# A two-layer SSD and mLSTM trunk on one core: how rows reach all partitions, and how modulation sums are taken

## The chip, the core and the metric

One core of a Trainium2 chip runs the whole program. The metric is device microseconds of one execution. Three executions of the kernel before were timed, and one was profiled.

## What is computed

The input is a residual stream of 256 tokens by 2048 channels and one conditioning vector `c`. There are two layers. Each one computes a modulation from `c`, applies an RMS norm with it, projects in, mixes tokens, projects out, gates and adds.

```
cond = silu(c)
for i in range(2):
    mod = cond @ ada_w[i] + ada_b[i]            # 2048 x 6144, one row
    shift, scale, gate = split(mod, 3)
    h = rmsnorm(x, norm_w[i]) * (1 + scale) + shift
    out = ssd_mixer(h, ...) if i == 0 else mlstm_mixer(h, ...)
    x = x + gate * out
return rmsnorm(x, final_norm_w)
```

The SSD mixer needs, for each of 64 heads, `exp(acs[t] - acs[s])` for all pairs of tokens of a chunk, where `acs` is a running sum over tokens. The mLSTM mixer needs `exp` of a like difference for each of 8 heads, and then `num = (q k^T * decay) @ v` with 512 value columns per head. All values are fp32.

## The kernel before, in words

Channels lie on the partitions (128) and tokens along the free axis (256). A weight tile of 128 x 2048 comes by a DMA from SyncE in two halves (`raw`, 512 KB each, six buffers). ScalarE rounds a half to `hi` (helper `act`, L73), VectorE takes the rest as `lo` (helper `vtt`, L81), and TensorE multiplies hi by hi, hi by lo and lo by hi (L253 to L255, or L264 to L266 for the value projection). A half is 24 matmuls of 256 columns. The buffers `hi` and `lo` are four each.

A list `items` fixes the order: weight tiles (`w`), modulation tiles (`a`) and norm chunks (`h`). For each half, the loop at the end prepares the next three halves (`prep`: loads, splits, modulation work, norm chunks), steps background work (`run_bg`) and then issues the matmuls. Background work is a list of Python generators, `gens`. One call of `run_bg` advances each of them to its next `yield`, and stops early after five of them when a tally of VectorE or ScalarE work is too high. `finish` steps all of them, whatever the tally, until the ones that it names are over. The framework then places the instructions on each engine's queue by the order of the source and its own model of durations, so the order on an engine can differ from the source's. Each engine's queue is run in order.

Modulation (`ada_work`): each of 12 groups of 1024 columns is accumulated by VectorE in `aacc` (L77, 16 steps; one buffer). Then, in the source directly behind the last step, TensorE transposes each of 8 blocks of 128 columns (L202), and ScalarE copies the transposed block onto itself with a running sum, which gives 8 columns of `asum`; the transposes of four blocks share one PSUM bank. VectorE adds the bias.

SSD (`gen_ssd`, one generator for each of 8 groups): `rows(j)` brings four rows of `acs` (1 KB each) to partition 0 of a tile `acb` by four DMAs from GpSimd (L567), and a GpSimd `partition_broadcast` copies them to all partitions (L569). `decay(j)` makes `E` of it on ScalarE. VectorE multiplies by `cbm`, TensorE multiplies with `X` (L612, L613). Then the squares of the result are summed for each token, GpSimd raises the sum to the power -0.5 (`stat_to_bcast`, L280, tile `rs`), VectorE spreads it to a diagonal-ready tile `dg`, and TensorE transposes it (`bcast`, L289). An output projection over groups begins with `finish` of these groups.

mLSTM (`gen_ml`, one for each of 8 heads): one row `G` goes the same way (L814, L815) to `Gb`. The value product (L848, L850) runs in four steps of two matmuls into a bank each, each followed by one VectorE operation (L77) and a `yield`.

The final norm's weights come by one DMA of a row and one `partition_broadcast` for each half (L320, L321).

Of the kernel before, what the change touches and what calls it, by code (L numbers as in the profile page):

```python
# [8 lines left out]
F32 = mybir.dt.float32  # L9
# [37 lines left out]
def trunk_kernel(ctx, tc, xt, vecs, ada, wdt, wss, wso, wgt, wml, wmo, fnw, result):  # L47
# [5 lines left out]
    sp = ctx.enter_context(tc.tile_pool(name="sp", bufs=2))  # L53
    pj = ctx.enter_context(tc.tile_pool(name="pj", bufs=4, space=PS))
    pm = ctx.enter_context(tc.tile_pool(name="pm", bufs=4, space=PS))

    uid = [0]

    def nm(s):
        uid[0] += 1  # L60
        return f"{s}{uid[0]}"
# [9 lines left out]
    def act(out, in_, func, **kw):  # L71
        charge("a", out, 0.833e-3, 0.1 + 0.09 * sum(isinstance(kw.get(k), bass.AP) for k in ("bias", "scale")))
        nc.scalar.activation(out, in_, func, **kw)  # L73

    def stt(out, a, s, b, op0, op1):
        charge("v", out, 1.04e-3, 0.07 + 0.06 * isinstance(s, bass.AP))
        nc.vector.scalar_tensor_tensor(out, a, s, b, op0, op1)  # L77

    def vtt(out, a, b, op):
        charge("v", out, 1.04e-3, 0.07)  # L80
        nc.vector.tensor_tensor(out, a, b, op)  # L81
# [16 lines left out]
    def vec(n, i=0, w=1):  # L98
        o, _ = VOFF[n]
        return V[:, o + i:o + i + w]  # L100
# [70 lines left out]
            run_bg()  # L171

    acc_tiles = {}
    known = set()

    def ada_work(it):
        layer, key, q, w = it["layer"], it["key"], it["q"], it["w"]
        per = 1024 // w
        if q == 0:
            acc_tiles[layer, key] = sp.tile([P, 1024], F32, tag="adaacc", name=nm("aacc"), bufs=1)  # L180
        acc = acc_tiles[layer, key][:, 0:w]
        for k in range(2 * per * q, 2 * per * (q + 1)):
            raw = it["raw"][(k // per) % 2][:, (k % per) * w:(k % per + 1) * w]
            if k == 0:
                vts(acc, raw, cond[:, 0:1], None, ALU.mult)
            else:
                stt(acc, raw, cond[:, k:k + 1], acc, ALU.mult, ALU.add)
        if q != it["nq"] - 1:
            return
        if isinstance(key, tuple):  # L190
            spans = [(4 * key[0] + 2 * key[1] + 16 * j, 2) for j in range(2)]
        elif key < 4:
            spans = [(4 * key, 4), (16 + 4 * key, 4)]
        else:
            spans = [(32 + 8 * (key - 4), 4), (36 + 8 * (key - 4), 4)]
        sm = sp.tile([P, 8], F32, tag="asum", name=nm("asum"))
        c = 0
        for o, n in spans:
            ps = misc()
            for b in range(n):  # L200
                sl = slice(b * P, (b + 1) * P)
                nc.tensor.transpose(ps[:, sl], acc[:, c * P:(c + 1) * P], ident)  # L202
                act(ps[:, sl], ps[:, sl], AF.Copy, accum_out=sm[:, c:c + 1])
                c += 1
            m = mod[layer][:, o:o + n]
            vtt(m, sm[:, c - n:c], vec(f"ab{layer}", o, n), ALU.add)
            known.update((layer, o + b) for b in range(n))
            if 16 <= o < 32:
                stt(amul[layer][:, o - 16:o - 16 + n], m, 1.0, vec(f"nw{layer}", o - 16, n), ALU.add, ALU.mult)

    def load(it):
        it["raw"] = {}
# [65 lines left out]
    def stat_to_bcast(v):  # L278
        r = sp.tile([P, 2], F32, tag="rs", name=nm("rs"))
        nc.gpsimd.tensor_tensor(r, v, nhalf, ALU.pow)  # L280
        return r
# [33 lines left out]
    class OutStat(RowStat):  # L315
        def prepare(self):
            self.w = []
            for i in range(2):
                w = sp.tile([P, 4, T], F32, tag="a4", name=nm("fnw")).rearrange("p b t -> p (b t)")
                nc.gpsimd.dma_start(w[0:1, :], fnw[:, 1024 * i:1024 * (i + 1)])  # L320
                nc.gpsimd.partition_broadcast(w, w[0:1, :])  # L321
                self.w.append(w)
            self.o = [wp.tile([P, D], F32, tag="y", name=nm("o"), bufs=4) for _ in range(2)]

# [146 lines left out]

    passes = set()

    # ------------------------------------------------------------ layer 0
    st0 = RowStat()
    for u in range(4):
        st0.add(u)
# [2 lines left out]
    dtT = cp.tile([P, 2, 64], F32, tag="dtT", name="dtT")  # L480
    acT = cp.tile([P, 3, 64], F32, tag="acT", name="acT")
    acs = cp.tile([P, T], F32, tag="rowA", name="acs")
    dsk = cp.tile([P, 32], F32, tag="dskh", name="dskh")
    vts(dsk, vec("dsk", 0, 32), 0.5, None, ALU.mult)
    cbm = {}
# [2 lines left out]
    def dt_done(banks):  # L488
        def g():
            bk = banks[0][:, 0:T]  # L490
            rw = sp.tile([P, 4, T], F32, tag="a4", name="dtrow")
            dt, tmp = rw[:, 0, :], rw[:, 1, :]
            vts(tmp, bk, vec("dtb"), None, ALU.add)
            softplus(tmp, dt)
            yield
            na = sp.tile([P, 1], F32, tag="na", name="na", bufs=1)
            act(na, vec("alog"), AF.Exp)
            vts(na, na, -1.0, None, ALU.mult)
            vts(tmp, dt, na, None, ALU.mult)
            for c in range(2):  # L500
                s = slice(c * P, (c + 1) * P)
                nc.vector.tensor_tensor_scan(acs[:, s], ones, tmp[:, s], 0.0, ALU.mult, ALU.add)
            cr = tmp[:, 0:P]
            vts(cr, acs[:, 0:P], -1.0, acs[:, P - 1:P], ALU.mult, ALU.add)
            yield
            p1, p2 = misc(), misc()
            for c in range(2):
                nc.tensor.transpose(p1[:, c * P:(c + 1) * P], dt[:, c * P:(c + 1) * P], ident)
                nc.tensor.transpose(p2[:, c * P:(c + 1) * P], acs[:, c * P:(c + 1) * P], ident)
            nc.tensor.transpose(p2[:, 2 * P:3 * P], cr, ident)  # L510
            vts(dtT, p1[:, 0:T].rearrange("p (c h) -> p c h", c=2)[:, :, 0:64],
                                    0.5, None, ALU.mult)
            nc.vector.tensor_copy(acT, p2[:, 0:384].rearrange("p (c h) -> p c h", c=3)[:, :, 0:64])
            yield
        held["dt"] = spawn(g())
# [44 lines left out]
    def gen_ssd(g):  # L560
        acb, E = [None, None], [None, None]

        def rows(j):
            acb[j] = sp.tile([P, 4, T], F32, tag="a4", name=nm("acb"))
            h0 = 8 * g + 4 * j
            for h in range(4):
                nc.gpsimd.dma_start(acb[j][0:1, h, :], acs[h0 + h:h0 + h + 1, :])  # L567
            fl = acb[j].rearrange("p h t -> p (h t)")
            nc.gpsimd.partition_broadcast(fl, fl[0:1, :])  # L569

        def decay(j):
            e = E[j] = sp.tile([P, 4, 384], F32, tag="e6", name=nm("E"))
# [60 lines left out]
        token_sq(xs, [v[:, tb:tb + 1] for tb in range(2)])  # L633
        vts(v, v, 1.0 / 512, 4 * EPS, ALU.mult, ALU.add)
        r = stat_to_bcast(v)
        yield
        rb = bcast(r)
        yield
# [100 lines left out]
        out.extend(extra[e:])  # L739
        items[start:] = out  # L740

    # ------------------------------------------------------------ layer 1
    m1 = len(items)
    eT = cp.tile([P, 2, 8], F32, tag="eT", name="eT")
    ncT = cp.tile([P, 2, 8], F32, tag="ncT", name="ncT")
    G = cp.tile([P, T], F32, tag="rowA", name="G")
    mnw = cp.tile([P, 32], F32, tag="mnwh", name="mnwh")
    vts(mnw, vec("mnw", 0, 32), 0.5, None, ALU.mult)

    def gates_done(banks):  # L750
        def g():
# [15 lines left out]
            nc.vector.tensor_tensor_scan(bc, for_scan, lf, 0.0, ALU.mult, ALU.add)  # L767
            vtt(ip, ip, bc, ALU.subtract)
            nc.vector.tensor_tensor_scan(G, ip, ip, 0.0, ALU.max, ALU.max)
            vtt(lf, bc, G, ALU.add)  # L770
            yield
            p1, p2 = misc(), misc()
# [38 lines left out]
    def gen_ml(h):  # L811
        yield from gate_ok(lambda: "gates" in held and held["gates"].over)
        Gb = sp.tile([P, T], F32, tag="gb", name=nm("Gb"))
        nc.gpsimd.dma_start(Gb[0:1, :], G[h:h + 1, :])  # L814
        nc.gpsimd.partition_broadcast(Gb, Gb[0:1, :])  # L815
        yield
        EP = sp.tile([P, 2, 384], F32, tag="e6", name=nm("EP"))
        e, pp = EP[:, 0, :], EP[:, 1, :]
# [24 lines left out]
        yield  # L843
        yield from gate_ok(lambda: h in v_t and h in to_t)
        v, to = v_t[h], to_t[h]
        for b in range(4):
            ps = misc()
            nc.tensor.matmul(ps[:, 0:T], v[:, 0, b * P:(b + 1) * P], pp[:, 0:T], start=True, stop=False,  # L848
                             skip_group_check=True)
            nc.tensor.matmul(ps[:, P:T], v[:, 1, b * P:(b + 1) * P], pp[:, T:384], start=False, stop=True,  # L850
                             skip_group_check=True)
            stt(to[:, b, :], to[:, b, :], 1.0, ps[:, 0:T], ALU.add, ALU.mult)
            yield
        ss = sp.tile([P, 2], F32, tag="ss2", name=nm("ss2"))
        sq = sp.tile([P, 4, T], F32, tag="e6", name=nm("sq"))
# [57 lines left out]
    add_out_pass(1, (6, 7), st2, True, st2.prepare, wmo, after=st2.write)  # L913
    interleave(m1, [a for cc in (4, 5) for a in ada_items(1, cc)], upto=40)

    # ------------------------------------------------------------ run
    halves = []
    for n, it in enumerate(items):
        if it["kind"] == "w":
# [8 lines left out]
    def prep(j):  # L928
        n, half = halves[j]
        it = items[n]  # L930
        if it["kind"] == "h":
            for k in it["ks"]:
                h_chunk(it["layer"], k)
            return
        while nload[0] < min(len(loads), it["ln"] + LOOK_LOAD):
            load(loads[nload[0]])
            nload[0] += 1
        if it["kind"] == "a":
            ada_work(it)
        else:  # L940
            with prio(*HP_SPLIT):
                split(it, half)
# [108 lines left out]
```

## Time and profile before

| | |
|---|---|
| median of three executions | 1790.29 us |
| the three | 1785.38, 1790.29, 1799.31 us |
| span of the profiled execution, first to last instruction | 1784.4 us |
| median less span | 5.9 us |
| TensorE busy | 1696.1 us |
| VectorE busy | 1295.9 us |
| ScalarE busy | 923.6 us |
| GpSimd busy | 97.4 us |
| mean granted TensorE clock | 0.979 of full |

The profiled execution's own time is its span and what lies around it; the table puts the latter at the difference to the median. A matmul's end is modelled and overlaps the next one's start, so busy shares are upper bounds of useful work, and the pace is read from starts.

### The profile page before, as it was taken

The numbers are of one execution on the slowest core, as the hardware profiler recorded it, in microseconds if no ns is written. First come the engines' busy times: TensorE is split into PE (matmuls) and PEld (weight loads), VectorE is DVE, ScalarE is ACT, GpSimd is POOL, SyncE is SP. The second block draws the span as 40 slices with busy tenths as digits, with TensorE's granted clock in tenths as the row PEclk, the third lists the DMA queues.
The fourth block names the chain that finished last, engine by engine and source line by source line (L and its number), as shares of the span: only waits on it lengthen the run. The fifth ranks groups of instructions, "written<-read, shape, count | busy, mean of one in ns | idle before, by whom it ended". The sixth has DMA issues, their size and how long they took to land.

```text
span 1784.4 us, 32951 instructions
## 1 busy us (share of the span) xinstructions
PE 1696.1 (95%) x13285; PEld 1633.0 (92%) x13285; DVE 1295.9 (73%) x1615; ACT 923.6 (52%) x1571; POOL 97.4 (5%) x127
## 2 busy tenths in 40 slices
PE   2999999999899899899999999999999999999997
PEld 2998999999899889899898989899989898989996
DVE  6789899999886789886777776646455555564554
ACT  3443557998553487445455445544345454454442
POOL 0000003222200020000000000000000000000000
PEclk6999999999999999999999999999999999999998
DMA  9988856566776885894666676545555555554551
GB/s 359 327 305 300 291 183 209 184 201 219 264 247 219 276 298 193 295 339 167 230 227 235 235 259 209 188 169 186 184 183 173 181 171 184 175 180 170 185 178 71
DMA packets 110377, 394.74 MB, mean 221 GB/s; under 512 B 14352, under 2 KB 14352, under 8 KB 110224
## 3 DMA queue, kind: packets, MB, share of 16 engines
q1 hardware_dynamic: 107856, 392.54, 64.5%
q8 instruction: 104, 1.70, 0.4%
q0 software_dynamic: 2368, 0.09, 0.1%
q14 instruction: 49, 0.40, 0.1%
HBM read 390.41 MB, written 2.10 MB: 220 GB/s over the span
## 4 chain that ended last, share of the span: by engine, by line
PE 68%; DVE 11%; issue 11%; DMA 5%; ACT 3%; POOL 1%; SPq 0%; ACTq 0%; POOLq 0%; DVEq 0%
PE pj L253 16%; PE pj L254 16%; PE pj L255 16%; DVE aacc L77 4%; DVE lo L81 4%; PE pj L264 3%; PE pj L265 3%; PE pj L266 3%; DMA raw<-in_ada 3%; PE ms L253 2%; PE ms L254 2%; PE ms L255 2%; ACT hi L73 1%; DMA raw<-in_wss 1%; PE ms L202 1%
## 5 line engine op out<-in xcount | busy, mean ns | idle before, releaser
L73 ACT ACTIVATE hi<-raw 128x1024 fp32r<-128x1024 f32 x548 | 580.9, 1062 | 719.9 <-PE pj L254 496.8
L81 DVE TENSOR_TENSOR lo<-raw,hi 128x1024 fp32r<-128x1024 f32 x548 | 670.0, 1225 | 321.9 <-ACT hi L73 318.9
L253 PE MATMUL pj<-hT,hi 128*128 128x256 f32 x2400 | 683.8, 285 | 4.3 <-ACT hT L73 4.3
L254 PE MATMUL pj<-hT,hi 128*128 128x256 f32 x2400 | 676.4, 282 | 0.5 <-DVE hT L77 0.5
L255 PE MATMUL pj<-hT,lo 128*128 128x256 f32 x2400 | 674.6, 281 | 1.3 <-DVE lo L81 1.3
L253 PEld LDWEIGHTS pj<-hT,hi 128*128 128x128 f32 x2400 | 456.7, 191 | 5.7 <-ACT hT L73 4.9
L254 PEld LDWEIGHTS pj<-hT,hi 128*128 128x128 f32 x2400 | 456.7, 190 | 1.7 <-issue 0.8
L255 PEld LDWEIGHTS pj<-hT,lo 128*128 128x128 f32 x2400 | 455.8, 190 | 2.1 <-DVE lo L81 1.7
L253 PE MATMUL pj<-y,hi 128*128 128x256 f32 x1024 | 292.2, 285 | 0.0
L254 PE MATMUL pj<-y,hi 128*128 128x256 f32 x1024 | 291.8, 285 | 0.0
L255 PE MATMUL pj<-y,lo 128*128 128x256 f32 x1024 | 291.4, 285 | 0.0
L77 DVE SCALAR_TENSOR_TENSOR aacc<-raw,cond,aacc 128x1024 f32<-128x1024 f32 x180 | 236.0, 1311 | 40.4 <-DMA raw<-in_ada 38.8
L253 PEld LDWEIGHTS pj<-y,hi 128*128 128x128 f32 x1024 | 197.2, 193 | 0.6 <-issue 0.3
L254 PEld LDWEIGHTS pj<-y,hi 128*128 128x128 f32 x1024 | 197.4, 193 | 0.0
L255 PEld LDWEIGHTS pj<-y,lo 128*128 128x128 f32 x1024 | 197.2, 193 | 0.0
L253 PE MATMUL ms<-hT,hi 128*128 128x256 f32 x448 | 127.2, 284 | 2.3 <-DVE park L81 2.0
L255 PE MATMUL ms<-hT,lo 128*128 128x256 f32 x448 | 126.2, 282 | 0.8 <-DVE lo L81 0.8
L254 PE MATMUL ms<-hT,hi 128*128 128x256 f32 x448 | 126.2, 282 | 0.0
L264 PE MATMUL pj<-hi,hT 128*128 128x512 f32 x256 | 101.8, 398 | 0.0
L265 PE MATMUL pj<-hi,hT 128*128 128x512 f32 x256 | 101.4, 396 | 0.0
L266 PE MATMUL pj<-lo,hT 128*128 128x512 f32 x256 | 101.2, 395 | 0.0
L253 PEld LDWEIGHTS ms<-hT,hi 128*128 128x128 f32 x448 | 85.2, 190 | 3.5 <-DVE park L81 2.6
(175 smaller groups left out, 1557.9 us busy)
## 6 DMA issues: line engine op xcount, KB each, us to landing
raw<-in_wml SPq DMA_DIRECT2D x256, 512.0 KB, 4.0
raw<-in_ada SPq DMA_DIRECT2D x192, 512.0 KB, 5.2
raw<-in_wss SPq DMA_DIRECT2D x160, 512.0 KB, 4.9
raw<-in_wso SPq DMA_DIRECT2D x64, 512.0 KB, 5.1
raw<-in_wmo SPq DMA_DIRECT2D x64, 512.0 KB, 3.6
xT<-in_xt SPq DMA_DIRECT2D x4, 512.0 KB, 6.2
out<-o SPq DMA_DIRECT2D x4, 512.0 KB, 4.0
raw<-in_wdt SPq DMA_DIRECT2D x2, 512.0 KB, 3.1
```

What stands on the lines that cost most here:

```text
L73: nc.scalar.activation(out, in_, func, **kw)
L77: nc.vector.scalar_tensor_tensor(out, a, s, b, op0, op1)
L81: nc.vector.tensor_tensor(out, a, b, op)
L202: nc.tensor.transpose(ps[:, sl], acc[:, c * P:(c + 1) * P], ident)
L253: nc.tensor.matmul(o, hi[:, w0:w0 + P], ah, start=first, stop=False, skip_group_check=True)
L254: nc.tensor.matmul(o, hi[:, w0:w0 + P], al, start=False, stop=False, skip_group_check=True)
L255: nc.tensor.matmul(o, lo[:, w0:w0 + P], ah, start=False, stop=last, skip_group_check=True)
L264: nc.tensor.matmul(o, ah[:, s], wh, start=(k == 0), stop=False)
L265: nc.tensor.matmul(o, al[:, s], wh, start=False, stop=False)
L266: nc.tensor.matmul(o, ah[:, s], wl, start=False, stop=(k == u.ktot - 1))
```

## The change

- `rows(j)`: the scan's result is written once to a DRAM scratch `acd`. One DMA from GpSimd per `j` then reads four rows of it and writes them to all 128 partitions (512 KB). The same for `G` with a scratch `Gd` (128 KB per head), and for the final norm's weights from the input itself. All uses of `partition_broadcast` on GpSimd are gone.
- Modulation sums: a background generator, spawned when a group of columns is accumulated. Its first step does nothing; its second step issues 8 matmuls with a block of `aacc` as weights and one column of ones as the moving side, and VectorE adds the bias from PSUM. `finish(sums)` stands ahead of the next group's first accumulation and ahead of each norm chunk.
- SSD: one more `yield` between `stat_to_bcast` and `bcast`.
- mLSTM value products: all eight matmuls of a head are issued in one step into two banks; after a `yield`, VectorE takes two operations of 512 columns with a `yield` behind each, in place of four of 256.

```diff
+    dr = ctx.enter_context(tc.tile_pool(name="dr", bufs=1, space=bass.MemoryType.DRAM))
...
         if q == 0:
+            finish(sums)
             acc_tiles[layer, key] = sp.tile([P, 1024], F32, tag="adaacc", name=nm("aacc"), bufs=1)
...
-        sm = sp.tile([P, 8], F32, tag="asum", name=nm("asum"))
-        c = 0
-        for o, n in spans:
+        def total():
+            yield
             ps = misc()
-            for b in range(n):
-                sl = slice(b * P, (b + 1) * P)
-                nc.tensor.transpose(ps[:, sl], acc[:, c * P:(c + 1) * P], ident)
-                act(ps[:, sl], ps[:, sl], AF.Copy, accum_out=sm[:, c:c + 1])
-                c += 1
-            m = mod[layer][:, o:o + n]
-            vtt(m, sm[:, c - n:c], vec(f"ab{layer}", o, n), ALU.add)
...
+            c = sum(n for _, n in spans)
+            for b in range(c):
+                nc.tensor.matmul(ps[:, b:b + 1], acc[:, b * P:(b + 1) * P], ones[:, 0:1], start=True, stop=True)
+            c = 0
+            for o, n in spans:
+                m = mod[layer][:, o:o + n]
+                vtt(m, ps[:, c:c + n], vec(f"ab{layer}", o, n), ALU.add)
...
+        sums.append(spawn(total()))
...
-                nc.gpsimd.dma_start(w[0:1, :], fnw[:, 1024 * i:1024 * (i + 1)])
-                nc.gpsimd.partition_broadcast(w, w[0:1, :])
+                nc.gpsimd.dma_start(w, fnw[:, 1024 * i:1024 * (i + 1)].partition_broadcast(P))
...
+            nc.gpsimd.dma_start(acd, acs[0:64, :])
...
-            for h in range(4):
-                nc.gpsimd.dma_start(acb[j][0:1, h, :], acs[h0 + h:h0 + h + 1, :])
-            fl = acb[j].rearrange("p h t -> p (h t)")
-            nc.gpsimd.partition_broadcast(fl, fl[0:1, :])
+            nc.gpsimd.dma_start(acb[j].rearrange("p h t -> p (h t)"),
+                                acd[h0:h0 + 4, :].rearrange("(o h) t -> o (h t)", o=1).partition_broadcast(P))
...
         r = stat_to_bcast(v)
+        yield
         yield
         rb = bcast(r)
...
+            nc.gpsimd.dma_start(Gd, G[0:8, :])
...
-        nc.gpsimd.dma_start(Gb[0:1, :], G[h:h + 1, :])
-        nc.gpsimd.partition_broadcast(Gb, Gb[0:1, :])
+        nc.gpsimd.dma_start(Gb, Gd[h:h + 1, :].partition_broadcast(P))
...
+        pv = [misc(), misc()]
         for b in range(4):
-            ps = misc()
-            nc.tensor.matmul(ps[:, 0:T], v[:, 0, b * P:(b + 1) * P], pp[:, 0:T], start=True, stop=False,
+            o = pv[b // 2][:, T * (b % 2):T * (b % 2) + T]
+            nc.tensor.matmul(o, v[:, 0, b * P:(b + 1) * P], pp[:, 0:T], start=(b % 2 == 0), stop=False,
...
-            stt(to[:, b, :], to[:, b, :], 1.0, ps[:, 0:T], ALU.add, ALU.mult)
+        yield
+        for i in range(2):
+            stt(to[:, 2 * i:2 * i + 2, :], to[:, 2 * i:2 * i + 2, :], 1.0, pair(pv[i]), ALU.add, ALU.mult)
             yield
...
         if it["kind"] == "h":
+            finish(sums)
```

## Rows read from the trace of the kernel before

**Rows 1.** Busy time by stretch: length, engines, granted clock, DMA share, GB/s.
```profile
400.00:450.00 50.00, 48.92 (x415) 47.41 (x415) 49.31 (x67) 43.69 (x109) 10.75 (x12) 1.00 0.66 224
...
900.00:1750.00 850.00, 849.84 (x6423) 812.25 (x6422) 517.40 (x642) 396.59 (x514) 16.92 (x24) 1.00 0.57 192
```

**Rows 2.** Waits of TensorE's matmuls, 45 to 1700 us: total us, times, longest.
```profile
PE ms L289 <- DVE dg L85: 13.0, 6, 6.7
PE ms L202 <- ACT ms L73: 8.0, 7, 3.9
...
PE ms L202 <- DVE aacc L77: 3.4, 5, 1.1
PE ms L612 <- DVE E L81: 2.9, 3, 2.1
```

**Rows 3.** GpSimd in order of time: start, duration, operation, idle before, its releaser.
```profile
275.91 4.21 POOL L567 DMA_DIRECT2D acb<-acs  x8 [258.17 <-DVE dtrow L85]
286.99 4.09 POOL L569 PARTITION_BROADCAST acb<-acb  x2 [6.87 <-issue]
...
467.20 1.52 POOL L569 PARTITION_BROADCAST acb<-acb  x1 [3.52 <-DMA acb<-acs]
476.56 0.73 POOL L280 TENSOR_TENSOR rs<-vs,nhalf 128x2 f32<-128x2 f32 x1 [7.84 <-issue]
```

**Rows 4.** VectorE in order of time, 464 to 478 us.
```profile
466.22 0.15 DVE L85 TENSOR_SCALAR vs<-vs 128x2 f32<-128x2 f32 x1
...
471.31 1.21 DVE L81 TENSOR_TENSOR lo<-raw,hi 128x1024 fp32r<-128x1024 f32 x1
477.33 0.48 DVE L85 TENSOR_SCALAR dg<-ones,rs 128x128 f32<-128x128 f32 x2 [4.81 <-POOL rs L280]
```

**Rows 5.** Short stretches at reduced clock, columns as in rows 1.
```profile
150.50:153.70 3.20, 3.20 (x17) 3.20 (x17) 2.36 (x6) 0.74 (x4) 0.00 (x0) 0.50 0.98 384
297.30:300.50 3.20, 3.20 (x19) 2.68 (x17) 3.13 (x5) 3.20 (x12) 0.41 (x1) 0.50 0.82 282
...
474.80:481.40 6.60, 3.64 (x17) 3.67 (x18) 4.07 (x6) 1.51 (x2) 0.73 (x1) 0.50 0.40 133
...
665.90:669.10 3.20, 3.20 (x16) 3.20 (x16) 2.69 (x3) 2.64 (x5) 0.00 (x0) 0.50 0.77 250
```

**Rows 6.** GpSimd's DMA issues of L567: ns min/median/max, first and last start.
```profile
L567 POOL DMA_DIRECT2D acb<-acs x64: 487/492/1282, 275.9 to 650.1; - x64
```

**Rows 7.** DMA issues: count, KB each, median us from issue to landing.
```profile
raw<-in_wss SPq DMA_DIRECT2D x160, 512.0 KB, 4.9
```

**Rows 8.** VectorE's products of the decay tile E, columns as in rows 6.
```profile
L81 DVE TENSOR_TENSOR E<-E,cbm x16: 1745/1751/2706, 294.6 to 697.6; 128x1536 f32<-128x1536 f32 x16
```

**Rows 9.** TensorE in order of time around one group's modulation sums.
```profile
145.74 0.27 PE L255 MATMUL ms<-hT,lo 128*128 128x256 f32 x1
...
148.57 0.61 PE L202 MATMUL ms<-ident,aacc 128*128 128x128 f32 x2 [1.05 <-ACT ms L73]
...
151.08 0.41 PE L253 MATMUL ms<-hT,hi 128*128 128x256 f32 x1
```

**Rows 10.** Waits of TensorE's weight loads, 45 to 1700 us.
```profile
PEld ms L202 <- ACT ms L73: 11.8, 18, 4.1
```

**Rows 11.** TensorE in order of time around two one-column matmuls.
```profile
934.44 0.28 PE L255 MATMUL pj<-hT,lo 128*128 128x256 f32 x1
934.55 0.50 PE L863 MATMUL ms<-ones,sq 128*128 128x1 f32 x4
...
935.12 0.28 PE L254 MATMUL pj<-hT,hi 128*128 128x256 f32 x1
```

**Rows 12.** TensorE in order of time around two transposes of 128 columns.
```profile
1011.63 0.28 PE L255 MATMUL pj<-hT,lo 128*128 128x256 f32 x1
1011.75 0.38 PE L289 MATMUL ms<-ident,dg 128*128 128x128 f32 x2
...
1012.09 0.28 PE L254 MATMUL pj<-hT,hi 128*128 128x256 f32 x1
```

More of the change, by code (lines that the diff above doesn't have):

```diff
@@ L173, in trunk_kernel @@
     acc_tiles = {}
+    sums = []
     known = set()
@@ L195, in ada_work @@
             spans = [(32 + 8 * (key - 4), 4), (36 + 8 * (key - 4), 4)]
-        sm = sp.tile([P, 8], F32, tag="asum", name=nm("asum"))
-        c = 0
-        for o, n in spans:
+        def total():
+            yield
             ps = misc()
-            for b in range(n):
-                sl = slice(b * P, (b + 1) * P)
-                nc.tensor.transpose(ps[:, sl], acc[:, c * P:(c + 1) * P], ident)
-                act(ps[:, sl], ps[:, sl], AF.Copy, accum_out=sm[:, c:c + 1])
-                c += 1
-            m = mod[layer][:, o:o + n]
-            vtt(m, sm[:, c - n:c], vec(f"ab{layer}", o, n), ALU.add)
-            known.update((layer, o + b) for b in range(n))
-            if 16 <= o < 32:
-                stt(amul[layer][:, o - 16:o - 16 + n], m, 1.0, vec(f"nw{layer}", o - 16, n), ALU.add, ALU.mult)
+            c = sum(n for _, n in spans)
[5 more added lines that the diff above has]
+                vtt(m, ps[:, c:c + n], vec(f"ab{layer}", o, n), ALU.add)
+                c += n
+                known.update((layer, o + b) for b in range(n))
+                if 16 <= o < 32:
+                    stt(amul[layer][:, o - 16:o - 16 + n], m, 1.0, vec(f"nw{layer}", o - 16, n), ALU.add, ALU.mult)
+            yield
+        sums.append(spawn(total()))
     def load(it):
@@ L482, in trunk_kernel @@
     acs = cp.tile([P, T], F32, tag="rowA", name="acs")
+    acd = dr.tile([64, T], F32, tag="acd", name="acd")
     dsk = cp.tile([P, 32], F32, tag="dskh", name="dskh")
@@ L746, in trunk_kernel @@
     G = cp.tile([P, T], F32, tag="rowA", name="G")
+    Gd = dr.tile([8, T], F32, tag="Gd", name="Gd")
     mnw = cp.tile([P, 32], F32, tag="mnwh", name="mnwh")
@@ L845, in gen_ml @@
         v, to = v_t[h], to_t[h]
+        pv = [misc(), misc()]
         for b in range(4):
-            ps = misc()
-            nc.tensor.matmul(ps[:, 0:T], v[:, 0, b * P:(b + 1) * P], pp[:, 0:T], start=True, stop=False,
+            o = pv[b // 2][:, T * (b % 2):T * (b % 2) + T]
+            nc.tensor.matmul(o, v[:, 0, b * P:(b + 1) * P], pp[:, 0:T], start=(b % 2 == 0), stop=False,
                              skip_group_check=True)
-            nc.tensor.matmul(ps[:, P:T], v[:, 1, b * P:(b + 1) * P], pp[:, T:384], start=False, stop=True,
+            nc.tensor.matmul(o[:, P:T], v[:, 1, b * P:(b + 1) * P], pp[:, T:384], start=False, stop=(b % 2 == 1),
                              skip_group_check=True)
-            stt(to[:, b, :], to[:, b, :], 1.0, ps[:, 0:T], ALU.add, ALU.mult)
+        yield
+        for i in range(2):
+            stt(to[:, 2 * i:2 * i + 2, :], to[:, 2 * i:2 * i + 2, :], 1.0, pair(pv[i]), ALU.add, ALU.mult)
             yield
```

## The prediction

> **What bounds the kernel now.** I read the stretches first, to see where TensorE is the limit and how firmly. From 900 to 1750 us it is busy for 849.84 of 850 us [rows 1]: there, only TensorE work that is added or taken away counts, and a wait elsewhere is worth nothing. Before 900 us the engines are balanced closely: from 400 to 450 us TensorE is busy for 48.92 of 50 us, VectorE for 49.31 and ScalarE for 43.69 [rows 1]. So a TensorE stall there is worth its length only where VectorE doesn't take its place. Second, the waits of TensorE, without the first 45 us, which wait for the first weights: the transposes of `bcast` wait 13.0 us in six places, those of the modulation sums 8.0 us for ScalarE and 3.4 us for the accumulation, and the decay products 2.9 us [rows 2]. All of these lines are touched by the change. Third, GpSimd's queue, since `bcast` waits for its power. It runs 97 us in all, but it idles at odd places: 6.87 us ahead of a `partition_broadcast`, put down to nothing but "issue", and 7.84 us ahead of a power that follows one [rows 3]. So each change between the two kinds of operation costs GpSimd some 7 us.
>
> **Part A, no `partition_broadcast`, and one more `yield` ahead of `bcast`.** At 466.22 us VectorE finishes the input of a power; the broadcast ends at 468.7; the power starts at 476.56, and TensorE gets its transpose from 477.33 on [rows 3, 4]. That one wait is the 6.7 us of the list [rows 2]. With no broadcast on GpSimd the power follows its input at once, and the `yield` lets the matmuls of a half (24) stand between. What is late next there: the half's `lo`, which ends at 471.31 + 1.21 = 472.52 [rows 4], where TensorE ran dry near 470.8 (477.5 less the 6.7), so about 1.7 us of the 6.7 stay. The waits also cost clock: 474.8 to 481.4 us and 665.9 to 669.1 us ran at 0.50, the 1.2 GHz level [rows 5], after TensorE had idled. In the first, the 3.6 us from the end of the wait on, at half pace, lose 1.8 us, in the second 3.2 us lose 1.6. All waits and this clock are 13.0 + 3.4 = 16.4 us. I take off the 1.7, and a further third of the rest (4.7), because VectorE's queue is so full in that stage that `dg` will stand behind splits and accumulations. A = -10.0 us, bounds -16.4 and -3 (only the longest wait, and only half of it).
>
> **Part B, the first decay rows.** The eight small DMAs are issued from 275.91 us on, and the two broadcasts run from 286.99 to 291.1 [rows 3]; the decay product comes late for TensorE by 2.9 us in three waits, 2.1 in the longest [rows 2], and 297.3 to 300.5 us runs at 0.50 behind it [rows 5], 1.6 us lost. After the change, the rows go to DRAM, and return in one DMA of 512 KB to 128 partitions. The trace has no such DMA from GpSimd. Issue: 0.49 us is the median for one row [rows 6]; above, I bound it by what it replaces, four issues and a broadcast, 4 x 0.49 + 2.0 = 4.0 us; I take 1 us, nearer to the row. Landing: 4.9 us, the median of the loads of the same size [rows 7]; for the write I take the same as a bound. So the first rows are there at 275.9 + 0.5 + 4.9 + 1 + 4.9 = 287.2, against 289 (half of the two broadcasts) before, and the second 1 us later in place of 291.1. The Trainium skill has a price for the read: in "DMA: Bandwidth & Descriptors", Anatomy of one DMA, 2.0 us and bytes over 436 GB/s, an estimate of 3.2 us for 512 KB, by which the first rows would come 1.7 us earlier still and the sum would gain up to 1 us. B = -3 us, bounds -4.5 and 0. The added 16 x 0.5 MB flow at DMA shares near 0.66 [rows 1], so they delay no load on the path; if that cover were gone, each would cost 1.4 us at the highest rate that these rows show (384 GB/s, [rows 5]).
>
> **Part C, VectorE beside GpSimd.** The decay product takes 1751 ns in the median and 2706 ns at most [rows 8]. I take the difference, 0.95 us, for the price of an overlap with a broadcast, GpSimd's longest operation [rows 3]; there are 16 broadcasts in the SSD stage. Not all meet a VectorE operation of this kind; half of them give 8 x 0.95 = 7.6 us of VectorE time, of which a third reaches TensorE. C = -2.5 us, bounds -5 and 0 (below nothing only by rival 2).
>
> **Part D, modulation sums.** From the matmul ahead of the first transpose to the second matmul behind the last, two one-column matmuls (four passes) take 935.12 - 934.44 = 0.68 us [rows 11], two transposes 0.46 [rows 12]. Less two matmuls of the main stream (0.12 each), that is 0.22 and 0.11 us apiece. 96 of them: 96 x 0.11 = +10.6 us of TensorE time, in full where TensorE is the limit and nearly so before. Against it stand the waits, 8.0 + 3.4 us [rows 2], and the clock after one of them, 0.50 from 150.5 to 153.7 us [rows 5], 1.6 us. In that place 145.74 to 151.08 us [rows 9], 5.34 us with four main matmuls in it, become 8 x 0.22 + 0.5 = 2.3 us. The weight loads show 11.8 us of waits for the same ScalarE copies [rows 10]; they overlap the matmuls' own by an unknown part. So D lies between +10.6 (no wait goes) and 10.6 - 11.4 - 11.8 - 1.6 = -14.2; I take -6, about the middle of what lies below zero, as the place above is a net -3 by itself. ScalarE loses 96 copies with their sums; I cost that at nothing, because VectorE and TensorE are fuller in that stage [rows 1].
>
> **Part E, value products in one burst.** The same eight matmuls for each head, in a stage in which TensorE has no gap [rows 1]: 0, bounds -1 and +1. VectorE's four operations become two, off the path. The final norm's broadcasts lie long before the end: 0.
>
> **The sum.** -10.0 - 3 - 2.5 - 6 = -21.5 us on a span of 1784.4. I keep the 5.9 us between span and median: 1790.3 - 21.5 = 1769.
>
> **Rivals.** *1, the wait is refilled.* VectorE is busy for 49.31 of 50 us [rows 1], and `lo` or the accumulation is the next late thing wherever a TensorE wait goes. Against it: at 471 to 477 us VectorE itself sat waiting for the power [rows 4]. Then A gives -6, B and C together -2, and D, its waits moved to `lo`, 0: 1782.
> *2, the broadcast DMA comes later than the old path (slower).* Its place is ScalarE's queue: the decay operations wait for `acb` there with the roundings to `hi` behind them, and the next power stands behind the issue on GpSimd. Today the first issue to the last broadcast is 15.2 us for two tiles [rows 3], so it decides from about 8 us for a tile. At 11 us, 3 us too many for each of 8 SSD groups cost 24 us, while D still gives about -6 and A half, -5... together +13 and the DMA share rises: 1803. For it: no row shows a GpSimd DMA with 128 rows. Against it: one-row issues took 0.49 us in the median and 1.28 at most beside a full VectorE [rows 6]. The Trainium skill speaks for it: "SBUF — State Buffer", SBUF: two separate sides, says that a DMA issued from GpSimd starves for descriptors while VectorE runs an operation that takes both ports; the row's median shows no such starving for single rows, and by that rule an issue would end with the VectorE operation, which is far below 3 us.
> *3, all waits go.* All lower bounds: -16.4 - 4.5 - 5 - 14.2 = -40: 1750.
> That the burst or the later sums don't appear as written, since the framework orders each queue itself, is possible and worth nothing by part E.
>
> **Chances.** Forecast 0.52 (its own spread 1760 to 1779), rival 1 0.28, rival 2 0.13, rival 3 0.07. The range 1750 to 1795 leaves out most of rival 2 and a little below. One per cent, 17.9 us, is about what a measurement of this kernel tells from no change, as its three runs span 13.9 us. Faster by over 1% is below 1772.4: some 0.7 of the forecast, rival 3 and a little of rival 1, 0.46. Slower by over 1%: rival 2, 0.13. Within: 0.41.
>
> **What would show it.** A: no idle of GpSimd put down to "issue", the power within 0.2 us of its input, TensorE's wait at L289 below 4 us in all. B: the first decay operation on ScalarE at or before 288 us. C: no decay product above 2 us. D: the sums as runs of 16 passes 0.11 us apart with no wait for ScalarE. E: TensorE still without a gap from 900 us on, and the same length of that stage. The prediction is wrong if VectorE's share before 900 us rises to the limit with TensorE's waits only renamed (rival 1), or if the GpSimd DMAs take longer to issue than 4 us or to land than 8 us (rival 2).

## The result, and the profile after

The changed kernel took 1803.61 us in the median of 8 runs (1796.05 to 1805.14), beside 1789.23 us for the kernel before on the same chip (8 runs): 1.0064 times as long, interval 1.0037 to 1.0090 (the ratio on record; the quotient of the two medians is 1.0080, so ratios here are good to about 0.2%). The forecast was 1769, the range 1750 to 1795. The profiled execution has a span of 1802.7 us, 18.3 more than before.

Busy time by stretch, first of the kernel before and then of the changed one (columns as in [rows 1]):

```profile
50.00:250.00 200.00, 193.08 (x1594) 188.51 (x1593) 175.33 (x205) 96.05 (x155) 0.00 (x0) 0.99 0.83 290
250.00:500.00 250.00, 235.18 (x1960) 226.68 (x1959) 236.13 (x302) 196.75 (x452) 61.27 (x75) 0.98 0.64 214
500.00:830.00 330.00, 312.68 (x2568) 306.08 (x2567) 271.35 (x339) 179.17 (x358) 12.84 (x14) 0.98 0.76 258
830.00:1010.00 180.00, 176.34 (x1267) 165.53 (x1266) 128.66 (x171) 84.78 (x120) 4.89 (x7) 0.98 0.67 226
```
```profile
50.00:250.00 200.00, 191.38 (x1543) 189.28 (x1543) 168.73 (x194) 84.86 (x101) 0.00 (x0) 0.95 0.83 293
250.00:500.00 250.00, 231.33 (x1935) 222.98 (x1934) 224.90 (x299) 190.66 (x423) 16.46 (x20) 0.98 0.71 237
500.00:830.00 330.00, 317.10 (x2604) 312.07 (x2603) 268.76 (x338) 168.66 (x289) 6.15 (x6) 0.97 0.76 260
830.00:1010.00 180.00, 169.32 (x1199) 158.02 (x1198) 125.35 (x166) 79.13 (x105) 2.40 (x4) 0.97 0.67 221
1010.00:1740.00 730.00, 730.00 (x5590) 701.52 (x5590) 432.27 (x517) 337.33 (x406) 9.35 (x15) 1.00 0.58 191
```

From 1010 us on TensorE has no gap, as before [rows 1], so all was lost earlier. Two sums show how. TensorE's idle time from 50 to 1010 us is 960 less the busy times: 960 - 917.28 = 42.7 us before and 960 - 909.13 = 50.9 us after, 8 more. And the granted clock is lower, by most before 250 us. Where it is below 1.00 it was at 0.50, the 1.2 GHz level: summed over windows of 1 us past 45 us (without a stretch that had begun earlier), TensorE spent 34.2 us at that level before and 61.4 us after, and was busy for 28.0 and 51.4 us of it. At half pace half of the busy time is lost (main matmuls of the changed kernel start 0.12 us apart at 89 us and 0.21 apart at 91 us): 23.4 / 2 = 11.7 us more. The first main matmul starts 2 us earlier (39.55 us, before 41.55). Together 8.2 + 11.7 - 2.0 = 17.9 of the 18.3 us. So nearly nothing is left for added TensorE work, on which part D had put 10.6 us.

The waits of TensorE's matmuls after, 45 to 1700 us, to be laid beside [rows 2]:

```profile
PE ms L616 <- DVE E L82: 9.7, 4, 5.9
PE ms L294 <- DVE dg L86: 7.7, 5, 3.4
PE ms L833 <- DVE qk L78: 6.7, 2, 4.0
PE ms L781 <- DVE gaterow L82: 3.6, 1, 3.6
PE pj L258 <- DVE xT L78: 3.5, 1, 3.5
PE ms L204 <- DVE aacc L78: 3.4, 1, 3.4
```

The waits for `dg` shrank from 13.0 to 7.7 us and those of the sums for ScalarE are gone (8.0), but the decay product now waits 9.7 us (before 2.9) and the qk product of two mLSTM heads 6.7 us (before, no such wait).

GpSimd after, in order of time (beside [rows 3]):

```profile
282.91 0.73 POOL L508 DMA_DIRECT2D acd<-acs  x1 [264.87 <-DVE dtrow L86]
285.30 1.11 POOL L572 DMA_DIRECT2D acb<-acd  x2 [1.66 <-DMA acd<-acs]
...
489.84 1.75 POOL L285 TENSOR_TENSOR rs<-vs,nhalf 128x2 f32<-128x2 f32 x1 [9.27 <-ACT hi L74]
```

No idle time is put down to "issue" ahead of a power any more. The broadcast DMA, and the decay product (columns as in [rows 6]):

```profile
L572 POOL DMA_DIRECT2D acb<-acd x16: 527/538/1027, 285.3 to 661.6; - x16
...
L82 DVE TENSOR_TENSOR E<-E,cbm x16: 1742/1751/1759, 300.0 to 697.4; 128x1536 f32<-128x1536 f32 x16
```

Its landing (columns as in [rows 7]):

```profile
acb<-acd POOLq DMA_DIRECT2D x16, 512.0 KB, 6.2
```

TensorE around the third group of sums, whose place before is [rows 9], and the stretch behind it, whose place before is the first of [rows 5]:

```profile
149.00 0.28 PE L260 MATMUL ms<-hT,lo 128*128 128x256 f32 x1
152.66 3.54 PE L204 MATMUL ms<-ones,aacc 128*128 128x1 f32 x16 [3.38 <-DVE aacc L78]
156.06 0.56 PE L258 MATMUL ms<-hT,hi 128*128 128x256 f32 x1
```
```profile
154.00:161.00 7.00, 7.00 (x34) 7.00 (x34) 4.76 (x12) 1.31 (x3) 0.00 (x0) 0.50 0.83 300
```

The eight blocks are 16 passes in a row; no main matmul stands between them any more, the wait is 3.38 us, and the clock, which had fallen within the wait (at about 151.5 us), is at 0.50 through 161 us, where before it was back after 3.2 us.

### The profile page after: what moved, and what is told of

Its sections match the earlier page's. It is cut to its first block, busy times and chain, and to the rows that moved or that the text cites. A ratio compares the mean times of both kernels' runs of the same rounds, so it can differ in the third digit from the quotient of the medians.

```text
span 1802.7 us, 32775 instructions
## 1 busy us (share of the span) xinstructions
PE 1709.1 (95%) x13381; PEld 1651.5 (92%) x13381; DVE 1283.0 (71%) x1599; ACT 895.2 (50%) x1379; POOL 38.0 (2%) x55
## 4 chain that ended last, share of the span: by engine, by line
PE 62%; DVE 13%; issue 11%; DMA 10%; ACT 3%; POOL 0%; SPq 0%; ACTq 0%; DVEq 0%; POOLq 0%
PE pj L258 15%; PE pj L260 15%; PE pj L259 15%; DMA raw<-in_ada 6%; DVE lo L82 4%; DVE aacc L78 4%; DMA raw<-in_wss 3%; PE pj L271 3%; PE pj L270 3%; PE pj L269 3%; PE ms L260 2%; PE ms L258 2%; PE ms L259 2%; ACT hi L74 1%; DVE xs L78 1%
## 5 line engine op out<-in xcount | busy, mean ns | idle before, releaser
L78 DVE SCALAR_TENSOR_TENSOR aacc<-raw,cond,aacc 128x1024 f32<-128x1024 f32 x180 | 230.6, 1281 | 47.9 <-DMA raw<-in_ada 46.4
```

## The experiments

Theory S: the broadcasts by DMA gain and the new sums lose. Rivals: D, the large DMAs come late; O, any change of the source makes the framework's planner put the rows of each engine in another order, worth several us either way. Every run is compared with the kernel before on its own chip. The last two columns are of one profiled execution each; those of b1 and c3 are the slowest of 12, 7 and 8 us above the median. The last one is the time at 1.2 GHz past 45 us, as above (before: 34.2).

| run | what | ratio to before, interval | span | us at 1.2 GHz |
|---|---|---|---|---|
| e1_bcast | broadcasts by DMA (rows, gates, final norm) | 0.9952 (0.9928, 0.9976) | 1784.7 | 30.7 |
| e2_sums | new sums | 1.0102 (1.0075, 1.0129) | 1807.7 | 61.4 |
| e3_yield | extra yield | 1.0029 (1.0008, 1.0050) | 1786.9 | 37.5 |
| e4_burst | value burst | 1.0021 (1.0003, 1.0038) | 1789.5 | 37.5 |
| b1_bsums | broadcasts, new sums | 1.0029 (1.0010, 1.0047) | 1798.4 | 58.0 |
| b2_nosums | whole change without new sums | 1.0027 (1.0012, 1.0041) | 1787.0 | 34.1 |
| b3_colnow | broadcasts, one-column sums at the old place | 0.9998 (0.9977, 1.0020) | 1785.6 | 51.2 |
| b5_own | whole change, the drain steps the sums alone | 1.0038 (1.0017, 1.0059) | 1789.5 | 47.8 |
| c2_colnow64 | b3 with 64 columns | 0.9966 (0.9949, 0.9983) | 1782.7 | 37.5 |
| c3_full64 | whole change with 64 columns | 1.0024 (1.0007, 1.0040) | 1801.5 | 51.2 |
| b4_trgen | b1 with the old transposes in the new place | 0.9972 (0.9959, 0.9985) | 1787.1 | 40.9 |
| c1_spread | broadcasts, one-column sums by twos | 0.9991 (0.9976, 1.0006) | 1783.3 | 41.0 |
| d1_noburst64 | c3 without the burst | 1.0010 (0.9992, 1.0028) | 1788.6 | 41.0 |
| d2_noyield64 | c3 without the extra yield | 1.0013 (0.9996, 1.0029) | 1788.0 | 44.4 |
| d3_spread64 | c1 with 64 columns | 0.9949 (0.9931, 0.9968) | 1777.6 | 37.5 |

**One part at a time.** Each applies the hunks of the diff that its name tells to the kernel before.

> Only the broadcasts are changed: acs, G and the final norm's weights reach all partitions by one DMA each, and partition_broadcast is gone; sums, yield and burst are as before. Theory S (the modulation sums cost what was lost, the broadcasts gain): 10 us below before, about 1780, no idle of GpSimd put down to issue. Rival D (the 512 KB DMAs come late and cost): 5 to 10 us above before, 1795 to 1800, with waits of the decay product (E) and of the first mLSTM heads on TensorE.

> Only the modulation sums are changed: one-column matmuls in a background generator, with finish ahead of norm chunks and of the next group. Theory S: 10 us above before, about 1800, of which 8 us are lost before 210 us (a wait on the accumulation with no main matmul between, and a half clock behind it). Rival D: 3 to 6 us below before, about 1785, as forecast for this part.

> Only the yield between the power and its transposes is added. Theory S: the wait at 471 us shrinks by a half's 2.8 us, 2 to 4 us below before. Rival O (any change of the source order moves the planner's order and that alone is worth several us in either direction): 5 us or more off before, in stretches where nothing that was edited runs.

> Only the value products are issued in one burst with two VectorE operations. Theory S: no change, within 2 us of before, TensorE without a gap from 910 us on. Rival O: the order of the first two heads changes, TensorE waits for qk near 915 and 970 us as in the changed kernel, 7 us above before.

The broadcasts gain 0.5%, the sums lose 1%, and the yield and the burst lose 0.2 to 0.3% each, though neither adds an instruction. For the broadcasts and the sums S held and D fell; for the yield and the burst S missed (it expected 2 to 4 us below before, and a change within 2 us), and for the yield O's 5 us are near. But e2 is not the price of the sums in the whole change. With `partition_broadcast` kept, GpSimd's queue, and then the first row of TensorE's waits, show what the new order does:

```profile
434.35 3.47 POOL L573 PARTITION_BROADCAST acb<-acb  x1 [3.11 <-DMA acb<-acs]
445.83 0.73 POOL L284 TENSOR_TENSOR rs<-vs,nhalf 128x2 f32<-128x2 f32 x1 [8.01 <-issue]
```
```profile
PE ms L293 <- DVE dg L85: 30.8, 7, 6.3
```

The powers now stand right behind broadcasts, and TensorE waits 30.8 us for `dg`, where it was 13.0 [rows 2]. In the whole change no broadcast is left on GpSimd, so the sums had to be judged on top of the DMA version.

**On top of the broadcasts by DMA.** b5 replaces `finish(sums)`, which steps every background generator until the sums are out:

```
+    def total_now():
+        for b in sums:
+            while b.step():
+                pass
```

b3 keeps the one-column matmuls, but issues them at once, without a generator.

> The kernel before with the broadcasts by DMA and the new sums; no extra yield in the statistics, no value burst. The broadcasts alone gave 1783.4 us, the whole change 1803.6. Theory S (the new sums cost what was lost, wherever they stand): 1800 to 1806, TensorE behind the broadcasts alone by about 10 us before 480 us. Rival V (the new sums cost the first 10 us, and the value burst the second 9 us, between 886 and 1003 us, as the heads wait longer for their qk product): 1792 to 1796, and no loss between 886 and 1003 us. Rival O (any change of the source lets the planner put the rows in another order, worth several us either way): anywhere from 1780 to 1805, without the same places.

> The whole change without the new sums (broadcasts by DMA, the extra yield, the value burst; sums by transposes and ScalarE copies as before). Theory S: 1783 to 1788, near the broadcasts alone. Rival V: 1792 to 1794, with the loss between 886 and 1003 us. Rival O: 1780 to 1805, with losses in other places than the whole change had.

> The broadcasts by DMA and one-column matmuls with ones that are issued where the old transposes stood: not deferred by a yield, not drained before the next chunk. S1 (the price of the passes themselves, 16 of 0.11 us for 8 transposes of 0.11 us less the waits for ScalarE): 1783 + 0 to 10, so 1783 to 1793. S2 (the deferral and the drain, which steps every other background generator too, shift the order of the whole program; the passes are cheap): 1780 to 1786, within 0.2% of the broadcasts alone. Rival O: 1780 to 1805.

> The whole change, except that the drain of the sums steps the sums' own generators alone, not every generator in the background list. S2 (the drain pushes the SSD and head work ahead in the program order): 1783 to 1793, most of the loss of 14 to 20 us against the broadcasts alone gone. S1 (the passes are the price) and rival V (the burst): 1800 to 1806, unchanged. Rival O: 1780 to 1805.

No theory took it all: the medians of b1 (1792.7 us) and b2 (1792.8) fit V, that of b3 (1788.7) fits S1, and b5 (1796.3) lies between S2 and the others. From e1 to b1 the sums add 0.8% and from e1 to b2 the yield and the burst add 0.75%; both together add 1.1% (the whole change), so the parts don't simply add up. The sums' part has one cause in the profile: b1's idle time from 50 to 1010 us is 45.6 us, e1's 45.0 (from the same windows as above), but b1 spends 27.3 us more at 1.2 GHz, worth up to 27.3 / 2 = 13.7 us, and its span is 13.7 us longer. In b3 the idle time falls to 37.2 us, 7.8 below e1's, of the 11.4 us of matmul waits that part D counted; the clock takes it back (51.2 - 30.7 = 20.5 us more at 1.2 GHz, up to 10.2 us).

**Is it the one-column form that the clock falls behind?** In four pairs little else changes in the source. c2, c3 and d3 give each matmul 64 columns of ones, of which one is read; b4 puts the old transposes and copies into the new generator; c1 issues two blocks, then yields.

```
-nc.tensor.matmul(ps[:, b:b + 1], acc[:, b * P:(b + 1) * P], ones[:, 0:1], start=True, stop=True)
+nc.tensor.matmul(ps[:, 64 * b:64 * b + 64], acc[:, b * P:(b + 1) * P], ones[:, 0:64], start=True, stop=True)
```

> The broadcasts by DMA and one matmul a block at once, as in the run before of this form (1.000 of before, 51 us of the trace past 45 us at 1.2 GHz, against 31 us for the broadcasts alone), but each against 64 columns of ones instead of one, of which one is read: the same matmuls, the same waits, more columns through the array. Theory C (TensorE's clock falls behind bursts of one-column passes, because almost nothing moves through the array in them): the stretches at 1.2 GHz shrink to 30 to 37 us and the time to 0.994 to 0.997 of before. Rival W (the clock falls because of the waits ahead of and around the burst, the columns don't matter): 48 to 58 us at 1.2 GHz, 0.999 to 1.003 of before, more if a 64-column pass takes longer than 0.11 us.

> The whole change with 64 columns of ones in the sums instead of one. The whole change stands at 1.0064 of before with 61 us at 1.2 GHz past 45 us, before has 34 us. Theory C: 34 to 42 us at 1.2 GHz and 0.999 to 1.003 of before (some 10 us back; the waits for the qk product of two heads stay). Rival W: 55 to 65 us at 1.2 GHz, 1.004 to 1.009.

> The broadcasts by DMA, and the old transposes with their ScalarE copies in the new place: deferred by a yield and drained as the new sums are. With one-column matmuls in this place it was 1.0029 of before and 58 us at 1.2 GHz; in the old place the old form gave 0.9952 and 31 us. Theory C (one-column passes): 0.994 to 0.998, 30 to 40 us at 1.2 GHz. Rival P (the place, with the drain, costs it, whatever form the sums have): 1.002 to 1.006 and over 50 us.

> The broadcasts by DMA and the one-column sums deferred, but two blocks at a time with other work between them, and drained alone. Theory C: no burst of 32 light passes is left, so 30 to 40 us at 1.2 GHz and 0.993 to 0.998 of before. Rival W: the wait for the accumulator stays, 45 to 58 us at 1.2 GHz, 0.999 to 1.004 of before.

> The broadcasts by DMA and the sums two blocks at a time, drained alone, against 64 columns of ones. The same against one column was 0.9991 of before, with 41 us at 1.2 GHz past 45 us, 10 of them behind the sums at 150 and 206 us. Theory C: 30 to 36 us at 1.2 GHz, 0.994 to 0.997, no worse than the broadcasts alone (0.9952), which would make it one of the fastest here. Rival W (columns don't matter where the wait is the same): 38 to 45 us, 0.998 to 1.001.

The second group, in the whole change and in c3, by stretch:

```profile
86.00:90.00 4.00, 3.93 (x35) 3.76 (x34) 1.83 (x5) 1.97 (x3) 0.00 (x0) 1.00 1.02 394
90.00:94.00 4.00, 4.00 (x23) 4.00 (x23) 3.61 (x6) 1.94 (x3) 0.00 (x0) 0.57 0.73 272
```
```profile
86.00:90.00 4.00, 4.00 (x36) 3.90 (x35) 1.67 (x2) 2.56 (x4) 0.00 (x0) 1.00 0.97 350
90.00:94.00 4.00, 4.00 (x36) 4.00 (x35) 3.68 (x9) 1.84 (x3) 0.00 (x0) 1.00 0.95 357
```

The same 16 matmuls, of one column and of 64 (ns min/median/max, first and last start):

```profile
L204 PE MATMUL ms<-ones,aacc x16: 242/250/250, 87.3 to 88.9; 128*128 128x1 f32 x16
```
```profile
L204 PE MATMUL ms<-ones,aacc x16: 275/275/294, 87.9 to 89.6; 128*128 128x64 f32 x16
```

63 more columns cost 0.1 us a group at most. Behind the one-column group the clock falls to 0.57 from 90 to 94 us, though the rows show TensorE busy for 3.93 of the 4 us before; behind the other it stays at 1.00. But this pair differs in one thing more, a gap of 0.07 us ahead of the one-column group. In b5 the same one-column group follows without a gap, and the clock stays:

```profile
86.00:90.00 4.00, 4.00 (x37) 4.00 (x36) 1.75 (x6) 2.14 (x3) 0.00 (x0) 1.00 1.00 335
90.00:94.00 4.00, 4.00 (x36) 4.00 (x35) 4.00 (x8) 3.53 (x6) 0.00 (x0) 1.00 0.85 328
```

A group with like idle time in both is the one at 428.2 us of the whole change and at 420.2 us of c3. TensorE waits 0.62 and 0.67 us shortly ahead of it and 0.56 and 0.51 us behind it, between the same instructions:

```profile
428.00:431.00 3.00, 2.44 (x23) 2.39 (x21) 3.00 (x8) 3.00 (x10) 0.30 (x1) 1.00 0.25 78
431.00:435.00 4.00, 4.00 (x23) 4.00 (x22) 3.31 (x7) 4.00 (x13) 1.38 (x1) 0.57 0.60 203
```
```profile
420.00:423.00 3.00, 2.49 (x23) 2.39 (x21) 3.00 (x8) 3.00 (x10) 0.32 (x1) 1.00 0.26 87
423.00:427.00 4.00, 4.00 (x37) 4.00 (x36) 3.32 (x7) 4.00 (x13) 1.37 (x1) 1.00 0.58 197
```

Counted over the groups of 16 in a row past 45 us that start at full clock (one column: the whole change, e2, b1, b3, b5, c1; 64 columns: c2, c3, d1, d2, d3): with 0.07 to 0.78 us of idle time in the 2 us before the group, the clock had fallen within 1.5 us of its end in 8 of 10 groups of one column and in none of 7 of 64 columns. Without idle time (0.01 us at most, and none in the 1 us behind) it had fallen in 1 of 34 and in none of 26. After waits of over 1 us it fell in all 6 groups of one column, most of which waited longer, and in 4 of 8 of 64. So the one-column form alone seldom went with a fall; the form with a short wait beside it mostly did. This is a count over the traces that there are, one execution a run, and not an experiment.

Over the kernel, 64 columns or transposes in place of one column make the time at 1.2 GHz smaller in each pair, and the ratio with it: b3 to c2 51.2 to 37.5 us and -0.32%, the whole change to c3 61.4 to 51.2 and -0.40%, b1 to b4 58.0 to 40.9 and -0.57%, c1 to d3 41.0 to 37.5 and -0.42%. That the time comes through the clock shows in the spans: within each pair idle time from 50 to 1010 us differs by 2.0 us at most, while half of the busy time at 1.2 GHz falls by 5.9, 3.8, 9.1 and 3.6 us, and the span by 2.9, 1.2, 11.3 and 5.7. The intervals of the two runs don't touch in the last two pairs and overlap a little in the first two. c3 kept more time at 1.2 GHz than theory C expected (34 to 42 us): what the longer waits of the whole change cost in clock stays, so W has a share there. W isn't wholly apart from the columns either: ahead of the group near 150 us TensorE waits 3.4 to 3.9 us for the accumulation in all runs with one column and 1.1 to 1.7 us in those with 64, as the order on the queues changes too. c1 came out at W's time (0.9991) with little more than C's clock; at 150 and 206 us its 16 passes stand in a row all the same. P fell, since the old form in the new place lost nothing of note against its own old place (0.9972 and 0.9952). In the changed kernel the one-column groups that start at 508.9, 620.5, 764.5, 993.2 and 1114.6 us, in the stream without any gap, are not followed by a fall.

**The burst or the yield.** d1 and d2 take one of them out of c3.

> The whole change with 64 columns of ones in the sums and without the value burst (broadcasts by DMA, extra yield, sums). With the burst it was 1.0024 of before and lost 7 us between 887 and 1002 us. Theory V (the burst costs that: the value products leave VectorE's queue early, VectorE then stands idle for the splits, and the next head's qk comes late for its product): no wait of TensorE for qk over 2.6 us, less than 3 us lost in that stretch, 0.996 to 1.000. Rival Y (the extra yield moves the later work too): 1.001 to 1.004, the loss in that stretch stays.

> The whole change with 64 columns of ones in the sums and without the extra yield (broadcasts by DMA, sums, value burst). Theory V: TensorE waits 3 to 5 us for qk at the second head, and 5 to 9 us are lost against the kernel before between the gates and 1003 us; 1.000 to 1.003. Rival Y: no such loss, 0.996 to 0.999.

VectorE after, from the first head's value products to the second head's qk (start, duration, operation, idle before, its releaser), then the product on TensorE:

```profile
929.50 1.28 DVE L78 SCALAR_TENSOR_TENSOR to<-to,ms 128x512 f32<-128x512 f32 x2
...
942.62 1.29 DVE L78 SCALAR_TENSOR_TENSOR aacc<-raw,cond,aacc 128x1024 f32<-128x1024 f32 x1 [2.02 <-DMA raw<-in_ada]
...
955.43 1.23 DVE L82 TENSOR_TENSOR lo<-raw,hi 128x1024 fp32r<-128x1024 f32 x1 [2.58 <-ACT hi L74]
...
973.95 0.68 DVE L78 SCALAR_TENSOR_TENSOR qk<-th,qk 128x512 f32<-128x512 f32 x1
...
974.78 1.62 PE L833 MATMUL ms<-qk 128*128 128x256 f32 x3 [4.02 <-DVE qk L78]
```

And before: the first head's last value product, the second head's qk, and its product, without a wait:

```profile
926.36 0.42 DVE L77 SCALAR_TENSOR_TENSOR to<-to,ms 128x256 f32<-128x256 f32 x1 [1.90 <-PE ms L850]
...
957.09 0.69 DVE L77 SCALAR_TENSOR_TENSOR qk<-th,qk 128x512 f32<-128x512 f32 x1
...
957.92 1.10 PE L827 MATMUL ms<-qk 128*128 128x256 f32 x4
```

With the burst the value products leave VectorE at 929.5 us instead of filling its gaps one by one, VectorE then stands in order behind splits and loads that aren't there yet (20.1 us of waits for `hi` from 900 to 1000 us, 13.0 before), and the next head's qk ends 4 us after TensorE has run out of other work, where before it came just in time. In the runs on the DMA version the wait for qk of the second head goes with the burst: it is there in b2, b5, c3 and d2 (3.1 to 4.0 us), and not, or with 0.5 us at most, in b1, b3, c1, d1 and d3. TensorE's idle time from 830 to 1010 us goes with it: 3.7 us before, 8.5 in c3, 4.0 in d1 and 8.2 in d2. So theory V holds for this wait, and rival Y falls for it; e4, without the DMA, has it at 1.1 us. In time the two runs differ from c3 by -0.14% and -0.11%, with intervals that overlap, and d1 came out slower than V expected: the yield costs about as much, in other places. Before 830 us d2 has 8 us less idle time than c3 (34.9 and 43.1), but not in the waits for `dg` (11.0 and 10.7 us). That share stays unsettled between a cost of the yield and a mere change of the planner's order.

The fastest version is d3: broadcasts by DMA, sums against 64 columns issued by twos, drained alone, no burst, no extra yield. It is 0.5% faster than the kernel before and about level with the broadcasts alone.

## Why the prediction was wrong, point by point

**The step that failed** is part D: it counted the passes and the waits, and took off a clock stretch behind one wait, but had no term for what the clock does around the passes themselves. The lower clock is 11.7 of the 18.3 us lost. A second step failed beside it, the yield and the burst (parts A and E): the order of the queues was called worth nothing, and the two cost 0.75% on top of the broadcasts (b2 against e1). Some pieces of D were near: where the new sums are issued without being deferred (b3), idle time fell by 7.8 us, and 16 passes came 0.11 us apart with no wait for ScalarE, as forecast. In the stream they cost 16 x 0.11 = 1.8 us a group beyond the neighbours. But D's +10.6 us for them was too much: in the stream before, from 970.5 to 974.3 us, eight transposes, most of them single, cost 1.6 us beyond the neighbours, not the 0.9 of [rows 12], so the passes add about 0.15 us a group or 2 us in all. The -6 became about +0.8% (14 us) on top of the broadcasts, for up to 13.7 us of which the clock is enough. That the form has a part in it was shown by the pairs, and the count adds that nearly all its falls had a wait beside them; the clock's share was worked out from the time at 1.2 GHz.

The Trainium skill says in "TensorE: Matmul & The Clock Gate", What's actually happening, that the gate follows how busy the engine has been. Around waits the trace agrees (at 0.50 from within the wait of 3.38 us through 161 us). It doesn't for the pair at 428 and 420 us, if the profile's busy time is taken for that activity: 2.44 of 3 us busy, and then 0.57, but 2.49 of 3 us, and then 1.00.

**Part A** had the first half of the mechanism right. The idle of 7 us ahead of powers is gone and the waits for `dg` fell by 5.3 us (forecast: 10 with the clock); its condition (below 4 us in all) wasn't met. What is left isn't VectorE's full queue behind the power, as the sum had it: in the three longest waits (3.4, 2.1 and 1.6 us) the power follows its input within 0.2 us, VectorE idles 0.6 to 0.9 us for it and makes `dg` at once. The input itself comes late there, behind a `lo`. Of the sum's pieces, 16.4 - 1.7 is 14.7, a third of which is 4.9, not 4.7. The extra yield, in A's sum a help, cost 0.3% by itself (e3).

**Part B** was wrong in sign. The rows do come earlier in the version with the broadcasts alone: issue at 275.53, first decay operation on ScalarE at 285.99, 10.5 us, against 13.1 before (275.91 to 289.01). In the whole change it took 11.3 us (282.91 to 294.23), from a start 7 us late, so 288 us was missed. The landing took 6.2 us, not the 4.9 of the weight loads. (The Trainium skill's "DMA: Bandwidth & Descriptors", Anatomy of one DMA, gave an estimate of 3.2 us; the measurement decides.) But TensorE waits longer for the decay product, 9.7 us and in e1 10.0, against 2.9: it runs out of other work at 288.4 us in e1 and only at 294.1 before. The planner puts the product earlier among the matmuls. Why it does wasn't tried.

**Part C** held in its sign: no decay product is above 1.76 us (before up to 2.71). Its worth in time wasn't tried alone. A without the yield, B and C came to -0.5% or some 8.6 us (e1), where their sum said 15.5.

**Part E** was mis-sized: 0 was forecast, the burst alone cost 0.2%, and in the whole change TensorE waits 4.0 us for qk at the second head. The stage after 1010 us is saturated, as said, but the first two heads before it aren't: from 900 to 1010 us TensorE was busy for 109.84 us before and 102.89 after. The averaged row over 850 us [rows 1] was full because VectorE came just in time there, and the forecast took that for slack.

**The rivals.** 1 came near A's size (-6, and 5.3 us of waits), not its reason and not the time; VectorE's share didn't rise (236.1 us of the 250 from 250 us on before, 224.9 after). 2 gave the right time, 1803, for a wrong reason: an issue took 0.54 us in the median and landed after 6.2, and no power waited behind one. So the rule of the Trainium skill's "SBUF — State Buffer", SBUF: two separate sides, by which such issues starve beside a VectorE operation that takes both ports, shows little here either: 1.03 us at most. 3 didn't occur.

## What to carry to other kernels

Before replacing transposes by matmuls of very few columns in a nearly full TensorE, look at the granted clock behind such passes in a trace that has them, above all where short waits stand beside them; here 64 columns cost 0.1 us a group at most and kept the clock behind short waits. Where a framework orders each queue, judge a part on top of the others, and expect an edit that moves no work to shift the time by 0.2 to 0.3%. A stage that reads 100% busy can still hang on an engine that delivers just in time: look at what its partner's queue would do when work there moves.

## What the runs showed of the hardware

TensorE's clock fell to 1.2 GHz behind 16 one-column fp32 matmuls in 8 of 10 places with 0.07 to 0.78 us of idle time just before them, in none of 7 such places where the 16 had 64 columns (1.7 us a group instead of 1.6), and in 1 of 34 places where one-column matmuls followed without idle time. A GpSimd DMA that reads 4 KB from DRAM into 128 partitions was issued in 0.54 us and landed after 6.2 us in the median, slower than a weight load of the same 512 KB (5.4 us in the same execution).
